# Moving layer 1's embedding products from the end of layer 0's attention to the start of layer 1's latent attention

## The chip, the cores and the metric

The kernel is one program on one core of a Trainium2 chip. The metric is device microseconds (us) of one execution, start to end. The core has five engines with a queue of instructions each: TensorE (PE; its weight loads are shown as PEld), VectorE (DVE), ScalarE (ACT), GpSimd (POOL) and SyncE (SP), which issues every DMA of this kernel.

## The reference

A trunk of two layers over 1024 tokens of width 1024. Layer 0 mixes with pooling and differential attention (six heads), layer 1 with latent attention (C, four heads) and a gated delta rule (D, four heads, chunks). After each mixer stands a gated embedding term:

```python
for i in range(DEPTH):
    hn = rmsnorm(h, norm_g[i])
    m = even_layer(hn, ...) if i % 2 == 0 else odd_layer(hn, ...)
    h = h + m
    h = h + jax.nn.sigmoid(h @ ple_w_gate[i]) * (p[i] @ ple_w_proj[i])
```

`p[i] @ ple_w_proj[i]` is the embedding product: 1024 tokens x 256 times 256 x 1024, one for each layer. It depends on inputs alone, so it may be done at any time before the end of its layer. In D each chunk needs the inverse of a unit triangular matrix:

```python
a_mat = eye + where(strict, kk * gamma * beta, 0)
sol = triangular_solve(a_mat, rhs, lower=True, unit_diagonal=True)
```

## The kernel before

Every product of weights and activations is three float32r matmuls (high by high, high by low, low by high parts; `mm3`, L142 to L144), so that the result is near float32. Weights come by DMA into one of 4 buffers named `raw`, ACT casts the high part `wh` (L134) and DVE subtracts for the low part `wl` (L135). Results gather in PSUM banks: two named `acc`, two `s`, two `x`, one `tr`, one `o`.

The program is written as generators that are stepped in turn; a scheduler then fixes at build time one order for every engine's queue. Each engine runs its queue in that order, and an instruction that waits holds up all behind it. Names of tiles carry a number for each use; the profile leaves the numbers out.

The stages that matter here, in order:

- Layer 0's attention heads. Beside the last head, `ple_both` makes the embedding products of both layers, 16 results of 128x512 for each layer, every one six matmuls. Each is copied from its bank into a tile `z` (L127 on ACT, L129 on DVE) and stored in DRAM as `ple` (L590). What is left when the head ends is drained by `step(*[ahead] * 32)`. Then `out_stage` (layer 0) takes the heads' results `cat` and the weights `w_out`; its first product waits for the last head, the weights and the banks.
- Layer 1's projections, `gdn_prep` (chunk matrices L into DRAM), and `gate_proj(1)` (`gp1`): eight gate products of 24 matmuls each, evacuated by ACT (L896) and DVE (L897).
- `block_solve`: 31 columns of 32x32 triangular inverses, one chain of 62 dependent DVE operations (L979, L981), whose result goes to DRAM as `xinv` (L982).
- `mla_prep(0)`: transposes of the first latent head's q and k (L1127, eight banks of four), each copied by ACT (L1128) and subtracted by DVE (L1129).
- `mla_attn` (C: scores L1144 to L1148, softmax L261 and L265, values L272) interleaved with `gdn` (D): `gdn_solve` loads `U` from `xinv` (L995), transposes it on DVE (L1005 to L1007) and finishes each inverse with small matmuls (L1012 to L1041); `gdn_half` runs the recurrence (L1073 to L1079).

Of the kernel before, what the change touches and what calls it, by code (L numbers as in the profile page):

```python
# [10 lines left out]
F32 = mybir.dt.float32  # L11
F32R = mybir.dt.float32r
# [9 lines left out]
P = 128  # L22
# [34 lines left out]
def trunk_kernel(ctx, tc, a, out, layers=2):  # L57
    nc = tc.nc
    v, s, g, pe, dma = nc.vector, nc.scalar, nc.gpsimd, nc.tensor, nc.sync
# [3 lines left out]
    wp = ctx.enter_context(tc.tile_pool(name="weights", bufs=9))  # L63
# [3 lines left out]
    pools = {}  # L67

    def nm(p):
        uid[0] += 1  # L70
        return f"{p}{uid[0]}"

    def open_pool(name, side="left"):
        st = ExitStack()
        p = st.enter_context(tc.tile_pool(name=name, bufs=1, side=side, reuse_waits="tile"))
        return st, p

    def T(tag, bufs, shape=(512,), dt=F32, pool=None, parts=P):
        return (pool or pools["y"]).tile([parts, *shape], dt, tag=tag, bufs=bufs, name=nm(tag))
# [4 lines left out]
    def bank(tag):  # L84
        return pp.tile([P, 512], F32, tag=tag, bufs=BANKS[tag], name=nm(tag))

    def xt():
        return T("x", 32, dt=F32R, pool=pools["x"])
# [35 lines left out]
    def copy(i, out_, in_):  # L124

        if i % 2 == 0:
            s.copy(out_, in_)  # L127
        else:
            v.tensor_copy(out_, in_)  # L129

    def split(hi, lo, src, scale=None):

        if scale is None:
            s.copy(hi, src)  # L134
            v.tensor_tensor(out=lo, in0=src, in1=hi.bitcast(F32), op=ALU.subtract)  # L135
        else:
            s.activation(hi, src, AF.Identity, scale=scale)
            v.scalar_tensor_tensor(out=lo, in0=src, scalar=scale, in1=hi.bitcast(F32),
                                   op0=ALU.mult, op1=ALU.subtract)
# [6 lines left out]
    def stage(src):  # L146
        raw = wp.tile([P, 512], F32, tag="raw", bufs=4, name=nm("raw"))
        dma.dma_start(raw, src)
        return raw

    def wload(ap, c0, n, nk=KC):

        res = []
        for k in range(nk):
            raw = wp.tile([P, 512], F32, tag="raw", bufs=4, name=nm("raw"))[:, :n]
            hi = wp.tile([P, 512], F32R, tag="hi", name=nm("wh"))[:, :n]
            lo = wp.tile([P, 512], F32R, tag="lo", name=nm("wl"))[:, :n]
            dma.dma_start(raw, ap[k * P:(k + 1) * P, c0:c0 + n])
            split(hi, lo, raw)
            res.append((hi, lo))  # L160
        return res
# [9 lines left out]
    def proj_T(act, w, j, h, ps, order=None):  # L171
        sl = slice(j * P, j * P + P)
        ks = order or list(range(len(w)))
        for i, k in enumerate(ks):
            xh, xl = act[k][h]
            mm3(ps, w[k][0][:, sl], w[k][1][:, sl], xh, xl, i == 0, i == len(ks) - 1)
# [115 lines left out]
    ple = [scratch("ple0"), scratch("ple1")]  # L292
# [52 lines left out]
    for k in range(KC):  # L345
        load_x(0, k, sums)
        raw = stage(a["ev_w_in"][k * P:(k + 1) * P, 0:512])
        hi, lo = [wp.tile([P, 512], F32R, tag=n, name=nm(n)) for n in ("hi", "lo")]
# [14 lines left out]
    for j, n in enumerate(("x", "x", "tr", "acc")):  # L363
        ps = bank(n)
# [202 lines left out]
        finish(1)  # L567
        yield

    def ple_both():  # L570

        for layer in range(layers):
            slots = [xt() for _ in range(8)]
            pT = [[None, None] for _ in range(2)]
            for h in range(2):
                for k in range(2):
                    hi, lo = slots[4 * h + 2 * k], slots[4 * h + 2 * k + 1]
                    split(hi, lo, stage(a["pT"][layer, k * P:(k + 1) * P, h * 512:(h + 1) * 512]))
                    pT[k][h] = (hi, lo)
            for gq in range(2):  # L580
                if gq == 0:
                    yield
                w = wload(a["ple_w_proj"][layer], 512 * gq, 512, nk=2)
                for j in range(4):
                    t = T("z", 2, (2, 512))
                    for h in range(2):
                        ps = bank("acc")
                        proj_T(pT, w, j, h, ps)
                        copy(h, t[:, h], ps)
                        dma.dma_start(ple[layer][4 * gq + j][h], t[:, h])  # L590
                    yield

    def fresh():
        return dict(Q=[], K=[], V=[], G=[])
# [1 line left out]
    def step(*gens):  # L596
        for it in gens:
            next(it, None)

    st = fresh()  # L600
    ahead = even_proj(0, st)
# [6 lines left out]
    for hd in range(6):  # L608
        at, late = even_attn(hd, st), ahead
        if hd < 5:  # L610
            st = fresh()
            ahead = even_proj(hd + 1, st)
        else:
            ahead = ple_both()
        step(at, at, ahead, late, done, at, at, ahead, at, at, ahead, at, ahead, at, at)
        done = at
    step(done)
# [115 lines left out]
    gq = row(ip, "gq", a["od_q_norm"].rearrange("o d -> (o d)"), 192)  # L733
# [234 lines left out]
    def block_solve(nt):  # L968

        xf = T("nx", 2, (1024,), pool=bp)  # L970
        N, X = [t.rearrange("p (j i) -> p j i", j=32) for t in (nt, xf)]
        tm = T("tm", 1, (256,), pool=bp)
        g.memset(xf, 0.0)
        g.memset(xf[:, 0:1024:33], 1.0)
        for j in range(31):

            nr, ncol = j + 1, 31 - j
            t = tm[:, 0:nr * ncol].rearrange("p (a i) -> p a i", a=nr)
            v.tensor_tensor(out=t, in0=X[:, 0:nr, j:j + 1].to_broadcast([P, nr, ncol]),  # L979
                            in1=N[:, j:j + 1, j + 1:32].to_broadcast([P, nr, ncol]), op=ALU.mult)  # L980
            v.tensor_tensor(out=X[:, 0:nr, j + 1:32], in0=X[:, 0:nr, j + 1:32], in1=t, op=ALU.subtract)  # L981
        dma.dma_start(xinv, xf)  # L982
# [126 lines left out]
            s.activation(ct, tr, AF.Identity, scale=onorm)  # L1109
            dma.dma_start(cat[1][4 + hd][h], ct)  # L1110

    def mla_prep(hd, st):
        for h in range(2):
            zq, zk = T("zq", 2, (4, 256), pool=mp), T("zq", 2, (4, 256), pool=mp)

            Q, K, V = T("Q", 3, (3, 512), F32R, mp), T("K", 3, (4, 512), F32R, mp), T("V", 4, pool=mp)
            for n, t in (("Q", Q), ("K", K), ("V", V)):
                st[n].append(t)
            dma.dma_start(zk, qkv[h][:, :, hd, 256:512])
            dma.dma_start(zq, qkv[h][:, :, hd, 0:256])  # L1120
            dma.dma_start(c3(V), qkv[h][:, :, hd, 512:640])
            yield
            for z, lo, dst, hb, lb, part in ((zk, 0, K, 2, 3, slice(0, P)), (zk, P, K, 0, 1, slice(0, P)),
                                             (zq, 0, Q, 1, 2, slice(0, P)), (zq, P, Q, 0, 0, slice(64, P))):
                ps = bank("acc")
                for c in range(4):
                    pe.transpose(ps[:, c * P:(c + 1) * P], z[:, c, lo:lo + P], ident)  # L1127
                s.copy(dst[:, hb, :], ps)  # L1128
                v.tensor_tensor(out=dst[part, lb, :], in0=ps[part], in1=dst[part, hb, :].bitcast(F32), op=ALU.subtract)  # L1129
            yield  # L1130
# [50 lines left out]
    w = wload(w_in, 0, 456)  # L1181
# [11 lines left out]
    qkvs, gp0, gp1 = both(), gate_proj(0), gate_proj(1)  # L1193
# [3 lines left out]
    nt = T("nx", 2, (1024,), pool=bp)  # L1197
    prep = iter(())
    for hd in range(H):
        w, zps = wload(w_in, 456 + 384 * hd, 384), []  # L1200
        for h in range(2):
            outs = []
# [1 line left out]
            step(cv, prep, cv, prep, cv, prep, prep)  # L1204
            prep = gdn_prep(hd, h, *outs)
    step(gp1, prep, gp1, prep, gp1, prep, prep)
    block_solve(nt)
    istack.close()
    istack, mp = open_pool("mla")
    PW[0], PBUFS[1] = T_, 1  # L1210
    PBUFS[0] = 2
    st = dict(Q=[], K=[], V=[])
    ahead = mla_prep(0, st)
    step(ahead, gp1, gp1, ahead, ahead, gp1, gp1, ahead, gp1)
    bstack.close()
    xstack.close()
    sstack, pools["scan"] = open_pool("scan", "right")
    astack, pools["y"] = open_pool("attn")

    def gdn():  # L1220
        parts = [(pair, h, {}) for pair in ((0, 1), (2, 3)) for h in range(2)]
        yield from gdn_load(*parts[0])
        for n, part in enumerate(parts):
            ahead = gdn_load(*parts[n + 1]) if n < 3 else iter(())
            for i, _ in enumerate(gdn_half(*part)):
                if i in (1, 3):
                    step(ahead)
                yield
        sstack.close()

    rec = gdn()
    for hd in range(H):
        at = mla_attn(hd, st)
        st = dict(Q=[], K=[], V=[])
        ahead = mla_prep(hd + 1, st) if hd < H - 1 else iter(())
        for i in range(9):
            step(at, rec)
            if i % 3 == 2:
                step(rec)
            if i in (3, 4, 6, 7):  # L1240
                step(ahead)
# [73 lines left out]
```

## Time and profile before

| | us |
|---|---|
| median of 3 runs | 1497.71 (1496.02 to 1498.46) |
| the profiled execution | 1490.0, its span 1488.3 |
| PE busy | 1419.7 (95% of the span), mean granted clock 0.99 |
| DVE busy | 1000.5 (67%) |
| ACT busy | 655.7 (44%) |
| embedding products drained after the last head of layer 0 | about 531 to 555 |
| `block_solve` on DVE | 1074.4 to 1104.5 |
| first softmax of the latent attention | 1105.5 |

Times within the span are us from its start. Most of the span PE has no gap; the page's slices show where it has. A row of the timeline reads: start, duration, engine, line, operation, output<-input, shape, count, and in brackets the idle time before it with what ended that. Matmul durations overlap: the distance between starts is what a stream of them costs.

### The profile page before, as it was taken

Reading aid. Unit: us, or ns where it says so; the run is one execution under the profiler, and the core shown is the slowest. Engines: PE = TensorE matmul, PEld = TensorE weight load, DVE = VectorE, ACT = ScalarE, POOL = GpSimd, SP = SyncE. Lnnn points to the kernel's source line nnn. Section 1 sums busy time; section 2 is a strip of 40 time slices with the busy share of each in tenths; the row PEclk is TensorE's granted clock in tenths of the full one; section 3 lists DMA queues with packets and bytes.
Section 4 is the critical chain, followed back from the end, with each engine's and each line's share of the span. In section 5 each row is a group of like instructions: output and inputs, shape, how many; then the busy total and the mean of one; then the engine's idle time right before and its main releaser. Section 6 shows DMA issues by size and latency. Waiting matters only on the chain. (4 is left out here: it accounts for less than half of the span.)

```text
span 1488.3 us, 22788 instructions
## 1 busy us (share of the span) xinstructions
PE 1419.7 (95%) x7494; PEld 1158.3 (78%) x7494; DVE 1000.5 (67%) x2939; ACT 655.7 (44%) x1642; POOL 206.2 (14%) x347
## 2 busy tenths in 40 slices
PE   7799999999999999999998999999889999999998
PEld 6578887888888778887886777888768788887786
DVE  7855666676767857356669789888577888643342
ACT  4415555565566751234454434444223446722220
POOL 3430101010101001012104441110000000000021
PEclk9999999999999999999999999999989999999999
DMA  5315233232335483334323442343455644353332
GB/s 166 95 51 141 56 101 79 78 90 68 100 86 148 134 276 94 107 120 152 118 41 131 167 154 99 99 133 123 138 162 183 212 140 149 114 156 99 120 114 85
DMA packets 131557, 181.52 MB, mean 122 GB/s; under 512 B 32496, under 2 KB 59248, under 8 KB 131440
## 3 DMA queue, kind: packets, MB, share of 16 engines
q1 hardware_dynamic: 131440, 180.08, 39.7%
q8 instruction: 59, 0.97, 0.3%
q14 instruction: 58, 0.48, 0.1%
HBM read 108.20 MB, written 52.95 MB: 108 GB/s over the span
## 5 line engine op out<-in xcount | busy, mean ns | idle before, releaser
L142 PE MATMUL acc<-wh,x 128*128 128x512 f32 (+1 forms) x576 | 231.6, 402 | 2.3 <-DVE g L454 1.9
L143 PE MATMUL acc<-wl,x 128*128 128x512 f32 (+1 forms) x576 | 229.9, 399 | 3.0 <-DVE wl L135 3.0
L144 PE MATMUL acc<-wh,x 128*128 128x512 f32 (+1 forms) x576 | 228.5, 397 | 0.0
L144 PE MATMUL acc<-x,wl 128*128 128x512 f32 x512 | 204.5, 400 | 3.3 <-DVE wl L135 3.3
L142 PE MATMUL acc<-x,wh 128*128 128x512 f32 x512 | 204.8, 400 | 1.9 <-ACT wh L134 0.9
L143 PE MATMUL acc<-x,wh 128*128 128x512 f32 x512 | 203.0, 397 | 0.0
L134 ACT CAST wh<-raw 128x512 fp32r<-128x512 f32 (+2 forms) x176 | 101.3, 599 | 80.2 <-PE acc L143 25.6
L135 DVE TENSOR_TENSOR wl<-raw,wh 128x512 fp32r<-128x512 f32 (+2 forms) x176 | 114.9, 674 | 28.6 <-ACT wh L134 25.9
L143 PEld LDWEIGHTS acc<-wl,x 128*128 128x128 f32 x576 | 109.4, 190 | 27.1 <-DVE wl L135 4.5
L142 PEld LDWEIGHTS acc<-wh,x 128*128 128x128 f32 x576 | 109.3, 190 | 25.7 <-issue 2.8
L144 PEld LDWEIGHTS acc<-wh,x 128*128 128x128 f32 x576 | 109.2, 190 | 22.3
L144 PEld LDWEIGHTS acc<-x,wl 128*128 128x128 f32 x512 | 96.5, 188 | 27.9 <-DVE wl L135 5.9
L142 PEld LDWEIGHTS acc<-x,wh 128*128 128x128 f32 x512 | 96.4, 188 | 25.0 <-ACT wh L134 1.3
L265 ACT ACTIVATE p<-p,mx 128x128 f32<-128x128 f32 (+7 forms) x128 | 99.4, 777 | 33.0 <-DVE mx L261 24.3
L143 PEld LDWEIGHTS acc<-x,wh 128*128 128x128 f32 x512 | 96.3, 188 | 21.5
L669 POOL TENSOR_TENSOR u<-hp,hp 128x512 f32<-128x512 f32 x32 | 43.5, 1358 | 486.9 <-DVE hp L135 205.7
L144 PE MATMUL acc<-hp,wl 128*128 128x512 f32 x256 | 101.6, 397 | 0.4 <-DVE wl L135 0.4
L143 PE MATMUL acc<-hp,wh 128*128 128x512 f32 x256 | 101.5, 396 | 0.0
L142 PE MATMUL acc<-hp,wh 128*128 128x512 f32 x256 | 101.4, 396 | 0.0
L261 DVE CUSTOM_DVE_ANT_0 p<-s,cst 128x512 f32<-128x512 f32 (+3 forms) x128 | 74.2, 586 | 29.2 <-PE s L523 15.6
L667 DVE SCALAR_TENSOR_TENSOR th<-th,ld 128x512 f32<-128x512 f32 x32 | 28.8, 899 | 73.7 <-ACT th L665 73.7
L450 ACT ACTIVATE z<-acc,rstd 128x256 f32<-128x256 f32 x48 | 22.7, 474 | 112.2 <-PE acc L144 112.2
(462 smaller groups left out, 2906.1 us busy)
## 6 DMA issues: line engine op xcount, KB each, us to landing
raw<-in_ev_w_in SPq DMA_DIRECT2D x56, 256.0 KB
Q<-sq SPq DMA_DIRECT2D x96, 128.0 KB
qkv<-zz SPq DMA_DIRECT2D x16, 640.0 KB
raw<-cat SPq DMA_DIRECT2D x32, 256.0 KB
ple<-z SPq DMA_DIRECT2D x32, 256.0 KB
raw<-in_ple_w_gate SPq DMA_DIRECT2D x32, 256.0 KB
ld<-ple SPq DMA_DIRECT2D x32, 256.0 KB
zq<-qkv SPq DMA_DIRECT2D x16, 512.0 KB
```

The costliest lines, as they stand in the source:

```text
L134: s.copy(hi, src)
L135: v.tensor_tensor(out=lo, in0=src, in1=hi.bitcast(F32), op=ALU.subtract)
L142: pe.matmul(ps, lh, rh, start=first, stop=False)
L143: pe.matmul(ps, lh, rl, start=False, stop=False)
L144: pe.matmul(ps, ll, rh, start=False, stop=last)
L261: v.tensor_tensor_reduce(out=pm[:, c * 512:c * 512 + n], in0=ps[:, 0:n], in1=mk, scale=-scale, scalar=prev, op0=ALU.add, op1=ALU.min, accu ...
L265: s.activation(pm[:, 0:w], pm[:, 0:w], AF.Exp, bias=prev, scale=-1.0, accum_out=sums)
L450: s.activation(z[:, t % 4, :], ps[:, 0:256], AF.Identity, scale=rstd[0][:, t:t + 1])
L667: v.scalar_tensor_tensor(out=th, in0=th, scalar=1.0, in1=r, op0=ALU.add, op1=ALU.mult)
L669: g.tensor_tensor(out=u, in0=hi.bitcast(F32), in1=lo.bitcast(F32), op=ALU.add)
```

## The change

`ple_both` becomes `ple_proj(layer, slot, outs)`. Layer 0's products stay beside the last head, with a `z` tile for each result: two results in flight where there were four. Layer 1's products become `fill`. Its first step (four loads of `pT`, split into a pool `embed` of their own) is stepped before `block_solve`; its eight others are stepped after the last gate product, with the first two `gdn_load` (two `gdn_solve`) called among them. Only then is the pool `attn` of the latent attention opened, in memory that `embed` has given back. Layer 1's results are copied by ACT alone, into the four `raw` buffers that weights and `pT` use too. `mla_prep(0)` takes the banks `s` and `x` by turns (four) in place of `acc` (two), and its steps are spread among the gate products.

```diff
-    def ple_both():
-        for layer in range(layers):
-            slots = [xt() for _ in range(8)]
...
-                    t = T("z", 2, (2, 512))
+    def ple_proj(layer, slot, outs):
+        pT = [[None, None] for _ in range(2)]
+        for h in range(2):
+            for k in range(2):
+                hi, lo = slot(), slot()
+                split(hi, lo, stage(a["pT"][layer, k * P:(k + 1) * P, h * 512:(h + 1) * 512]))
+                pT[k][h] = (hi, lo)
+        yield
+        for gq in range(2):
+            w = wload(a["ple_w_proj"][layer], 512 * gq, 512, nk=2)
+            for j in range(4):
+                for h in range(2):
+                    ps, t = bank("acc"), outs()
+                    proj_T(pT, w, j, h, ps)
+                    copy(h * (1 - layer), t, ps)
+                    dma.dma_start(ple[layer][4 * gq + j][h], t)
+                yield
...
-            ahead = ple_both()
+            ahead = ple_proj(0, xt, lambda: T("z", 2, (2, 512))[:, 0])
...
-    def mla_prep(hd, st):
+    def mla_prep(hd, st, banks=("acc",)):
...
-                ps = bank("acc")
+                ps = bank(banks[nb % len(banks)])
+                nb += 1
...
-    block_solve(nt)
     istack.close()
     istack, mp = open_pool("mla")
+    fstack, fp = open_pool("embed")
+    fill = ple_proj(1, lambda: T("pT", 8, dt=F32R, pool=fp), lambda: wp.tile([P, 512], F32, tag="raw", bufs=4, name=nm("ple")))
+    step(fill)
+    block_solve(nt)
...
-    ahead = mla_prep(0, st)
-    step(ahead, gp1, gp1, ahead, ahead, gp1, gp1, ahead, gp1)
+    ahead = mla_prep(0, st, ("s", "x"))
+    step(ahead, gp1, gp1, ahead, gp1, ahead, gp1, ahead, gp1)
...
-    astack, pools["y"] = open_pool("attn")
...
     rec = gdn()
+    step(fill, fill, rec, fill, fill, fill, rec, fill, fill, fill)
+    fstack.close()
+    astack, pools["y"] = open_pool("attn")
```

In the changed kernel the lines from `mla_prep` on are two lower (L1125 are its transposes, L1127 its subtractions), those from `out_stage` to `gdn_half` four lower (L893 for L897, L975 and L977 for L979 and L981, L1008 for L1012).

What moves in the queues, at three places. First PE, from the last gate products on. Before, `acc_11570` and `acc_11599` are the fourth and fifth gate product, 24 matmuls each; `zq` are the first head's k and q:

```order
L144 MATMUL acc_11570<-wh_11302,x_7604 128x512
L142 MATMUL acc_11599<-wh_11260,x_7269 128x512
...
L144 MATMUL acc_11599<-wh_11302,x_7788 128x512
L1127 MATMUL acc_11628<-cst,zq_11563 128x128 x4
L1127 MATMUL acc_11635<-cst,zq_11563 128x128 x4
...
L142 MATMUL acc_11664<-wh_11260,x_7269 128x512
...
L272 MATMUL o_11901<-V_11566,pt_11904 128x128
L1012 MATMUL acc_11830<-wk_11816,L_11804 32x32
L1147 MATMUL s_11992<-K_11565,Q_11564 128x384
```

Now `acc_11528` is the seventh gate product and `acc_11585` the eighth, `acc_11631` the first embedding result, `acc_11661` the fourth, `acc_11754` the fifth:

```order
L144 MATMUL acc_11528<-wh_11110,x_7596 128x512
L1125 MATMUL s_11463<-cst,zq_11398 128x128 x4
L1125 MATMUL x_11470<-cst,zq_11398 128x128 x4
...
L142 MATMUL acc_11585<-wh_11068,x_7077 128x512
...
L142 MATMUL acc_11631<-pT_11306,wh_11620 128x512
...
L144 MATMUL acc_11661<-pT_11324,wl_11627 128x512
L1146 MATMUL s_11993<-K_11400,Q_11399 128x256
L1008 MATMUL acc_11697<-wk_11683,L_11671 32x32
...
L1037 MATMUL acc_11742<-U_11672,kw_11680 128x128 x4
L142 MATMUL acc_11754<-pT_11306,wh_11620 128x512
```

The first transposes stood behind five gate products and now stand behind seven. The first solve (L1012, now L1008) stood among attention matmuls and now stands ahead of twelve of the sixteen embedding results.

Second DVE, inside `block_solve` (`tm` and `nx` are its tiles). Before, seven columns in:

```order
L981 TENSOR_TENSOR nx_11491<-nx_11491,tm_11492 128x6x26
L979 TENSOR_TENSOR tm_11492<-nx_11491,nx_9539 128x175
L1129 TENSOR_TENSOR K_11565<-acc_11628,K_11565 128x512
L981 TENSOR_TENSOR nx_11491<-nx_11491,tm_11492 128x7x25
L1129 TENSOR_TENSOR K_11565<-acc_11635,K_11565 128x512
```

Now:

```order
L977 TENSOR_TENSOR nx_11330<-nx_11330,tm_11331 128x6x26
L1127 TENSOR_TENSOR K_11400<-s_11463,K_11400 128x512
L975 TENSOR_TENSOR tm_11331<-nx_11330,nx_9347 128x175
L1127 TENSOR_TENSOR K_11400<-x_11470,K_11400 128x512
L977 TENSOR_TENSOR nx_11330<-nx_11330,tm_11331 128x7x25
```

The subtraction of the first transposed bank stands at the same column as before, one operation earlier.

Third DVE, at the end of layer 0's last head (L546 scales the head's last output `o`, which PE then transposes on L553; `wl` are `w_out`'s low parts). Before:

```order
L543 TENSOR_TENSOR ony_5895<-ony_5895,hrstd_149 128x4
L546 SCALAR_TENSOR_TENSOR o_5588<-o_5588,ony_5895,g_5018 128x128 x4
L135 TENSOR_TENSOR wl_6301<-raw_6299,wh_6300 128x512
L129 COPY z_6007<-acc_6017 128x512
L135 TENSOR_TENSOR wl_6307<-raw_6305,wh_6306 128x512
```

Now:

```order
L135 TENSOR_TENSOR wl_6121<-raw_6119,wh_6120 128x512
L543 TENSOR_TENSOR ony_5898<-ony_5898,hrstd_149 128x4
L135 TENSOR_TENSOR wl_6127<-raw_6125,wh_6126 128x512
L546 SCALAR_TENSOR_TENSOR o_5589<-o_5589,ony_5898,g_5018 128x128 x4
L129 COPY z_6005<-acc_6004 128x512
```

Four of `w_out`'s subtractions that stood behind L546 now stand ahead of it (the last two are shown).

More of the change, by code (lines that the diff above doesn't have):

```diff
@@ L568, in even_attn @@
         yield
-    def ple_both():
-        for layer in range(layers):
-            slots = [xt() for _ in range(8)]
[L574 to L584, printed above, removed]
-                    t = T("z", 2, (2, 512))
-                    for h in range(2):
-                        ps = bank("acc")
[L588 to L591, printed above, removed]
+    def ple_proj(layer, slot, outs):
[15 more added lines that the diff above has]
+                yield
     def fresh():
@@ L1110, in gdn_half @@
             dma.dma_start(cat[1][4 + hd][h], ct)
-    def mla_prep(hd, st):
+    def mla_prep(hd, st, banks=("acc",)):
+        nb = 0
         for h in range(2):
@@ L1124, in mla_prep @@
                                              (zq, 0, Q, 1, 2, slice(0, P)), (zq, P, Q, 0, 0, slice(64, P))):
-                ps = bank("acc")
+                ps = bank(banks[nb % len(banks)])
+                nb += 1
                 for c in range(4):
```

## The prediction, before the run

> **What bounds the kernel now.** I read the page first: busy shares and slices, for where PE, the busiest engine, has room.
>
> ```profile
> PE 1419.7 (95%) x7494; PEld 1158.3 (78%) x7494; DVE 1000.5 (67%) x2939; ACT 655.7 (44%) x1642; POOL 206.2 (14%) x347
> PE   7799999999999999999998999999889999999998
> ```
>
> PE is the bound nearly everywhere, so moving products helps only if they leave a place where PE is full and land where it is empty. The place they leave, by stretches of PE's work on the tile `acc` (columns: stretch, length, busy, count, clock, DMA share, GB/s), and the first product of the output stage from PE's timeline:
>
> ```profile
> 531.80:555.10 23.30, 22.83 (x97) 1.00 0.83 276
> 555.17 0.50 PE L142 MATMUL acc<-x,wh 128*128 128x512 f32 x1 [0.51 <-ACT z L127]
> ```
>
> From the last head's end to the output stage PE does 96 or so embedding matmuls without a gap, at full clock. That is layer 1's share, and it can go. The place they go to, by PE's timeline, and by stretches of all engines (length, then PE, PEld, DVE, ACT, POOL busy with counts, clock, DMA share, GB/s):
>
> ```profile
> 1061.56 0.48 PE L142 MATMUL acc<-wh,x 128*128 128x512 f32 x1
> 1072.88 0.60 PE L1127 MATMUL acc<-cst,zq 128*128 128x128 f32 x4
> 1074.54 0.66 PE L1127 MATMUL acc<-cst,zq 128*128 128x128 f32 x4 [1.06 <-DVE gz L897]
> 1078.92 1.97 PE L1127 MATMUL acc<-cst,zq 128*128 128x128 f32 x8 [3.72 <-DVE K L1129]
> 1105.88 0.44 PE L1144 MATMUL s<-K,Q 128*128 128x384 f32 x1 [1.71 <-DVE mx L261]
> 1110.62 0.80 PE L272 MATMUL o<-V,pt 128*128 128x128 f32 x2 [3.54 <-DVE r L1152]
> 1111.34 0.31 PE L1012 MATMUL acc<-wk,L 32*32 32x32 f32 x2
> 1072.80:1081.70 8.90, 4.12 (x22) 3.20 (x20) 7.10 (x22) 2.92 (x5) 0.00 (x0) 0.70 0.51 160
> 1104.20:1111.30 7.10, 1.80 (x6) 1.05 (x6) 2.54 (x15) 1.93 (x6) 0.00 (x0) 0.71 0.83 237
> 1116.30:1160.00 43.70, 42.32 (x459) 35.94 (x457) 33.48 (x146) 17.35 (x37) 3.33 (x8) 1.00 0.61 189
> 1160.00:1306.00 146.00, 141.22 (x1162) 123.78 (x1162) 113.22 (x449) 83.20 (x182) 1.69 (x4) 1.00 0.49 153
> ```
>
> PE is empty for 4.8 of 8.9 us around the first transposes and for 5.3 of 7.1 us before the first solve, some 10 us. After 1116 it is full again (42.3 of 43.7). So the room is under half of the products' time, and whether even that is used hangs on the queues. The chain through this place runs on DVE and SP, by their timelines:
>
> ```profile
> 1074.40 0.18 DVE L979 TENSOR_TENSOR tm<-nx,nx 128x31 f32<-128x31 f32 x1
> 1077.92 0.34 DVE L979 TENSOR_TENSOR tm<-nx,nx 128x175 f32<-128x175 f32 x1
> 1078.18 0.68 DVE L1129 TENSOR_TENSOR K<-acc,K 128x512 fp32r<-128x512 f32 x1
> 1104.27 0.21 DVE L981 TENSOR_TENSOR nx<-nx,tm 128x31 f32<-128x31 f32 x1
> 1104.55 0.33 SPq L982 DMA_DIRECT2D xinv<-nx  x1
> 1107.29 0.32 SPq L995 DMA_DIRECT2D U<-xinv  x1
> 1105.53 0.28 DVE L261 CUSTOM_DVE_ANT_0 p<-s,cst 128x128 f32<-128x128 f32 x1
> 1109.35 0.42 DVE L261 CUSTOM_DVE_ANT_0 p<-s,cst 128x256 f32<-128x256 f32 x1 [3.52 <-DMA gate<-gz]
> ```
>
> `block_solve` holds DVE for 30.1 us (1074.40 to 1104.48). From its end to the first solve matmul on PE pass 6.8 us (1104.55 to 1111.34): store, load of `U`, transposes on DVE.
>
> **The change part by part.** The unit: the fourth and fifth gate products are 48 matmuls and take 11.32 us (1061.56 to 1072.88), so 0.236 each; a gate product is 5.66, an embedding result of six 1.41, layer 1's sixteen 22.6 us.
>
> *Early, what is removed.* 22.6 us of PE leave the drain. Late next is the last head's end. DVE now has four more subtractions of `w_out` ahead of L546, by the listings.
>
> ```profile
> 530.58 1.14 DVE L546 SCALAR_TENSOR_TENSOR o<-o,ony,g 128x128 f32<-128x128 f32 x4
> 531.08 0.50 PE L553 MATMUL tr<-cst,o 128*128 128x128 f32 x2
> 531.64 0.68 DVE L135 TENSOR_TENSOR wl<-raw,wh 128x512 fp32r<-128x512 f32 x1
> 533.59 0.32 SPq L590 DMA_DIRECT2D ple<-z  x1
> 536.90 0.59 ACT L127 COPY z<-acc 128x512 f32<-128x512 f32 x1 [2.78 <-DMA ple<-z]
> ```
>
> At 0.6 us each (their distance when queued) L546 starts about 2.4 us later, at 533, and L553 at 533.6. One embedding result stands behind it (1.4), and its bank and the next wait for copies into `z`: a store holds its tile for 3.3 us (533.59 to 536.90), and with two results in flight instead of four that is 4.0 us for two results where PE needs 2.8, so the last ones wait about 1 us. The output stage then starts near 536.0 instead of 555.2: a gain of 19.2. Bounds: 22.6 if neither costs anything; 15 if the staging of `cat` and `w_out`, at a DMA share of 0.83 in this stretch, is late by another 4. The second half of `cat` and the loads of x are needed only from the third product chain on, 11 us later, and are covered by it; without that cover they would cost up to 4, the same bound.
>
> *Late, the DVE wait.* PE now runs four gate products before the first transposes: 1061.56 + 4 x 5.66 = 1084.2. Transposes, ACT's copy and the queue bring the first subtraction L1127 to 1085.4. DVE reaches it after the twelfth operation of `block_solve` (1078.3) and one subtraction of `pT` (0.6), at 1078.9, and stands for 6.5 us with all the rest of the inverse behind it. From there before took 26.3 us (1078.18 to 1104.48) with eight subtractions and two gate evacuations in it; now one more evacuation and two `wl` (three times 0.6), less about 1 us of small waits that go, so 27.1. `block_solve` ends at 1112.6, plus 6.8: the first solve can start at 1119.4. If the stall were nothing it would be 1112.9.
>
> *Late, what PE has until then.* After 1084.2: transposes 4.0, a wait for the `acc` bank of the sixth gate product (ACT evacuates it only behind four casts, DVE behind four subtractions) about 2.5, the eighth gate product 5.7, four embedding results 5.7, ten score matmuls 1.7: until 1104. The other twelve results stand behind L1008 in PE's queue, so PE is empty for 15.4 us. The four banks for the transposes cost nothing and gain the two waits of 1.06 and 3.72, but only where PE is not waiting for more; they are in the sum through these times.
>
> *Late, the solves.* Before, solves ran with attention matmuls between their steps; now nothing stands between.
>
> ```profile
> 1123.36 0.21 PE L1012 MATMUL acc<-wk,L 32*32 32x32 f32 x1
> 1129.95 1.06 PE L1041 MATMUL acc<-U,kw 128*128 128x128 f32 x8
> 1121.37 2.05 PE acc L1041 x16
> 520.40 0.44 SPq L158 DMA_DIRECT2D raw<-in_ev_w_out  x1
> 523.76 0.62 ACT L134 CAST wh<-raw 128x512 fp32r<-128x512 f32 x1 [0.46 <-DMA raw<-in_ev_w_out]
> ```
>
> A solve takes 7.5 us from end to end (1123.36 to 1130.9), of which PE works about 4 (estimate: L1041 2.05, the three smaller steps together as much). So: first solve 7.5; four results 5.7 and 1 for the clock after the wait; two recurrence matmuls 0.5; then two results whose weights come late. Their `raw` buffers are the tiles of the results just stored: one store (3.3), one load to cast (3.4, 520.40 to 523.76), cast and subtraction 1.3, in all 8 us after the first copy, so 5.8 us pass for 2.8 us of work; second solve 7.5; six results 8.5. That is 36.5 us: the fill ends at 1155.9. The ends: 25.7 if PE waits for nothing, 42 if each solve takes 9 and the weights 3 more.
>
> *Late, who waits.* Attention's pool is opened in `embed`'s memory, and DVE's first softmax stands behind all of this. It starts at 1155.9 instead of 1105.5: 50.4 later. Given back: two solves are done (2 x 4 of PE, which is full from there on), and the 3.5 us that the second softmax waited for a gate's store. Lag 38.9. Eight copies go from DVE to ACT, 0.59 each (the row at 536.90); ACT is busy for 17.4 of 43.7 us after 1116 and has that room, without it they would cost 4.7. SP's queue gets layer 1's 24 transfers: two `pT` loads stand ahead of the last load for `block_solve`, 0.9 us at 0.44 an issue, covered because the inverse starts behind the fifth gate product (done 1072.9) anyway, else 0.9; the stores of the first four results are issued before 1105, ahead of `xinv`'s turn. POOL's order is unchanged.
>
> The rest of the attention, full before (141.2 of 146), can give back a few us at most; I take none. Sum: 38.9 - 19.2 = +19.7 on the profiled 1490.0, so 1509.7. The profiled execution is 7.7 below the median of the runs; on the median 1497.7 it is 1517.4.
>
> The clock beside this:
>
> ```profile
> 1082.16 0.63 PE L143 MATMUL acc<-wl,x 128*128 128x512 f32 x1
> 1082.58 0.63 PE L144 MATMUL acc<-wh,x 128*128 128x512 f32 x1
> 1083.36 0.40 PE L143 MATMUL acc<-wl,x 128*128 128x512 f32 x1
> 1083.59 0.39 PE L144 MATMUL acc<-wh,x 128*128 128x512 f32 x1
> ```
>
> After the gap that ended at 1078.92 matmuls came 0.42 apart, by 1083.36 0.23 apart: some 4 us at near half rate, 2 lost. I take half of it after the long wait, since the solve itself covers the rest. The Trainium skill, "TensorE: Matmul & The Clock Gate", Part 1, has the array at half rate after an idle window of about 3.4 us, until about 3.4 us of work. By that rule the long wait costs 1.7 and the sum is 0.7 higher; the trace agrees with it here. The same page asks for no gaps of over 3 us between bursts, and by that the change, which puts products into a gap, should win: that is the first rival.
>
> **The rivals.**
>
> *The queue's order does not bind, and PE never runs dry (faster).* Place: L1008. The price is the plain work: 1084.2 + 4.0 + 5.7 + 22.6 + 1.7 + 8 + 1 = 1127.2 for the fill's end; lag 1127.2 - 1105.5 - 8 - 3.5 = 10.2, less 19.2 gives -9, so 1488.7. It needs L1008 to start by about 1106 and something to run between the solves' steps; with the rest packed, each us of later start costs one, and the sign turns at 1115. Against it: `block_solve` cannot end before 1078.9 + 27.1 = 1106 even without the stall, and the 6.8 follow.
>
> *All follow-on waits are small (no change).* No stall on DVE (-6.5), solves at PE's 4 us (-7), weights in time (-3), no clock loss (-1), the full 22.6 early (-3.4): 19.7 - 20.9 = -1.2, 1496.5. For it: ACT and DMA have room. Against it: it needs all five.
>
> *The early gain is not had.* The drain covers the staging of the output stage (DMA 0.83); if that then binds, only 15 less a further wait remain: with a gain near 3 the sum is +36, 1534. Against it: `cat` loads move ahead of the head's end in SP's queue, and four of w_out's weights are split before L546.
>
> **How the numbers follow.** Likeliest, 0.72: slower by 19.7, own range +9 (half of the five savings) to +30 (early 15, solves 9, no softmax wait given back): 1507 to 1528. First rival 0.13, second 0.09, third 0.06. A measurement here tells about 0.2%, 3 us, from nothing. Faster: the first and a little of the second, 0.15; the same: most of the second, 0.06; slower: 0.79. The range 1490 to 1529 leaves out most of the third and the lower half of the first, about 0.13, and what nobody listed.
>
> **What would show it.** Right: PE's first output product near 536; DVE idle some 6 us before the first L1127; `xinv` stored near 1112 - 19; PE idle over 10 us before the first L1008; first softmax near 1156 - 19. Wrong: L1008 starting within 2 us of the scores before it, or the solves' steps taking 4 us. A wait at the output stage's first product, with DMA as releaser, would speak for the third rival.

## The result and the profile after

The changed kernel takes 1513.31 us (median of 4 runs, 1512.56 to 1514.02), the kernel before 1496.87 (4 runs, 1492.54 to 1498.46). The ratio is 1.0114, with a 95% interval of 1.0092 to 1.0137: slower by 16.4 us. The profiled execution takes 1512.76 us with a span of 1511.0, against 1490.0 and 1488.3 before.

The page's busy row and PE's slices:

```profile
PE 1424.3 (94%) x7494; PEld 1163.0 (77%) x7494; DVE 996.6 (66%) x2931; ACT 660.6 (44%) x1650; POOL 205.1 (14%) x347
PE   7799999999999899999999999999659999999998
```

The same number of matmuls, and a hole in two slices (6 and 5, from 1058 to 1133 us) where before stood 8 and 8. The hole by stretches (length, busy time and count of PE, PEld, DVE, ACT, POOL, granted clock, DMA share, GB/s):

```profile
1085.70:1099.80 14.10, 0.02 (x1) 0.01 (x1) 7.39 (x26) 0.00 (x0) 0.00 (x0) 0.65 0.85 289
1099.80:1110.50 10.70, 7.21 (x72) 6.37 (x72) 4.89 (x30) 0.59 (x1) 0.31 (x1) 0.51 0.62 186
1110.50:1116.80 6.30, 6.30 (x31) 5.04 (x29) 1.44 (x12) 2.70 (x5) 0.53 (x1) 1.00 0.45 140
1116.80:1125.90 9.10, 4.39 (x13) 3.21 (x13) 1.68 (x3) 2.40 (x6) 0.00 (x0) 0.81 0.35 105
1125.90:1134.25 8.35, 5.74 (x72) 5.21 (x73) 2.27 (x7) 0.99 (x2) 0.30 (x1) 0.80 0.26 94
1134.25:1142.70 8.45, 8.45 (x39) 6.87 (x38) 1.91 (x15) 3.52 (x6) 0.53 (x1) 1.00 0.38 132
```

In this order: PE stands empty; the first solve; four results; two results with late weights; the second solve; six results. Only the stretches with results alone are full. The events, by the timelines of PE and DVE:

```profile
535.05 0.40 PE L142 MATMUL acc<-x,wh 128*128 128x512 f32 x1
545.38 0.68 DVE L645 TENSOR_TENSOR t<-acc,ld 128x512 f32<-128x512 f32 x1
1064.61 0.60 PE L1125 MATMUL s<-cst,zq 128*128 128x128 f32 x4
1065.99 0.69 DVE L1127 TENSOR_TENSOR K<-s,K 128x512 fp32r<-128x512 f32 x1 [7.14 <-ACT K L1126]
1069.74 1.09 PE L1125 MATMUL s<-cst,zq 128*128 128x128 f32 x4 [3.23 <-DMA zq<-qkv]
1093.35 0.21 DVE L977 TENSOR_TENSOR nx<-nx,tm 128x31 f32<-128x31 f32 x1
1099.52 0.48 DVE L1001 STREAM_TRANSPOSE wk<-U 32x32 f32<-32x32 f32 x4 [5.96 <-DMA U<-xinv]
1099.82 0.28 PE L1008 MATMUL acc<-wk,L 32*32 32x32 f32 x2 [14.10 <-issue]
1121.00 0.80 PE L142 MATMUL acc<-pT,wh 128*128 128x512 f32 x1 [4.19 <-ACT wh L134]
1142.24 0.29 DVE L261 CUSTOM_DVE_ANT_0 p<-s,cst 128x128 f32<-128x128 f32 x1 [3.95 <-PE acc L144]
```

DVE waits 7.14 us for the late transposes with most of `block_solve` behind it; PE then waits 14.10 us for `block_solve`'s result (through the load of `U` and its transposes on DVE) with twelve of the sixteen results behind L1008; the first softmax comes at 1142.24, behind all of them. Its row ends on one of the last product matmuls (`<-PE acc L144`): the pool `attn` lies in memory that the products' operands hold until then, so no softmax runs beside PE's gap either.

One measure serves for all that follows: the late stage, from the last `gdn_prep` product (`x<-cq,ck`) to latent attention's last gated output (`og`), by the groups of these tiles (count, min/median/max in ns, first and last start). Before, then after:

```profile
L948 PE MATMUL x<-cq,ck x64: 274/275/276, 910.9 to 1061.5; 128*128 128x128 f32 x64
L1162 DVE SCALAR_TENSOR_TENSOR og<-o,r,gt x32: 330/350/352, 1112.0 to 1302.6; 128x128 f32<-128x128 f32 x32
```
```profile
L944 PE MATMUL x<-cq,ck x64: 275/275/275, 891.6 to 1042.0; 128*128 128x128 f32 x64
L1160 DVE SCALAR_TENSOR_TENSOR og<-o,r,gt x32: 338/350/353, 1146.9 to 1325.8; 128x128 f32<-128x128 f32 x32
```

It is 241.1 us before and 283.8 after: 42.7 more. A second profiled execution of the changed kernel gives 285.1, so this measure repeats to about 1 us. What comes behind it (185 to 186 us) and what lies between the output stage's first subtraction and it (494 to 498) is the same in every kernel here. The way up to that subtraction is not so steady: 545.38 in one execution of the changed kernel, 540.93 in the other.

### The profile page after: what moved, and what is told of

It reads as the page before. It is cut to its first block, busy times and chain, and to the rows that moved or that the text cites. A ratio compares the mean times of both kernels' runs of the same rounds, so it can differ in the third digit from the quotient of the medians.

```text
span 1511.0 us, 22755 instructions
## 1 busy us (share of the span) xinstructions
PE 1424.3 (94%) x7494; PEld 1163.0 (77%) x7494; DVE 996.6 (66%) x2931; ACT 660.6 (44%) x1650; POOL 205.1 (14%) x347
## 4 chain that ended last, share of the span: by engine, by line
PE 68%; DVE 15%; DMA 7%; ACT 6%; issue 3%; POOL 1%; SPq 0%; DVEq 0%; ACTq 0%; POOLq 0%
PE acc L144 16%; PE acc L142 16%; PE acc L143 16%; PE o L272 4%; PE s L522 1%; PE tr L279 1%; DVE wl L135 1%; PE s L523 1%; DVE p L261 1%; PE acc L1037 1%; DMA raw<-in_xT 1%; DMA raw<-in_ev_w_in 1%; DMA raw<-cat 1%; ACT p L265 1%; PE x L944 1%
## 5 line engine op out<-in xcount | busy, mean ns | idle before, releaser
L144 PE MATMUL acc<-wh,x 128*128 128x512 f32 (+1 forms) x576 | 228.1, 396 | 0.0
L142 PE MATMUL acc<-x,wh 128*128 128x512 f32 x480 | 192.9, 402 | 2.5 <-ACT z L127 1.1
L144 PE MATMUL acc<-x,wl 128*128 128x512 f32 x480 | 192.2, 401 | 3.1 <-DVE wl L135 3.1
L143 PE MATMUL acc<-x,wh 128*128 128x512 f32 x480 | 190.1, 396 | 0.0
L144 PEld LDWEIGHTS acc<-wh,x 128*128 128x128 f32 x576 | 109.1, 189 | 22.5
L265 ACT ACTIVATE p<-p,mx 128x128 f32<-128x128 f32 (+7 forms) x128 | 99.4, 777 | 33.3 <-DVE mx L261 22.6
L144 PEld LDWEIGHTS acc<-x,wl 128*128 128x128 f32 x480 | 90.5, 189 | 26.5 <-DVE wl L135 5.7
L142 PEld LDWEIGHTS acc<-x,wh 128*128 128x128 f32 x480 | 90.7, 189 | 24.3 <-DVE z L129 1.3
L143 PEld LDWEIGHTS acc<-x,wh 128*128 128x128 f32 x480 | 90.6, 189 | 20.6
L144 PE MATMUL acc<-hp,wl 128*128 128x512 f32 x256 | 101.2, 395 | 0.0
L663 DVE SCALAR_TENSOR_TENSOR th<-th,ld 128x512 f32<-128x512 f32 x32 | 32.4, 1014 | 72.6 <-ACT th L661 72.5
L450 ACT ACTIVATE z<-acc,rstd 128x256 f32<-128x256 f32 x48 | 22.8, 475 | 112.1 <-PE acc L144 112.0
```

Source lines behind the costliest of these rows:

```text
L142: pe.matmul(ps, lh, rh, start=first, stop=False)
L143: pe.matmul(ps, lh, rl, start=False, stop=False)
L144: pe.matmul(ps, ll, rh, start=False, stop=last)
L265: s.activation(pm[:, 0:w], pm[:, 0:w], AF.Exp, bias=prev, scale=-1.0, accum_out=sums)
L450: s.activation(z[:, t % 4, :], ps[:, 0:256], AF.Identity, scale=rstd[0][:, t:t + 1])
L663: v.scalar_tensor_tensor(out=th, in0=th, scalar=1.0, in1=r, op0=ALU.add, op1=ALU.mult)
```

## The experiments

Theory: the loss is one of order in PE's queue. The products stand behind a solve that cannot start, the solves run with nothing between their steps, and the weights of the last products come late. Rivals: the products are slow in this place whatever stands around them; or the reordered transposes cost the time, not the products. A part of the theory is left untested: no run gives attention memory of its own, so what it loses by the pool alone is not known.

All times, each ratio to the kernel before in the same comparison (its median lay between 1490.3 and 1496.9 in the four comparisons), and the late stage:

| kernel | us | ratio, 95% interval | late stage |
|---|---|---|---|
| before | 1496.87 | 1 | 241.1 |
| changed | 1513.31 | 1.0114 (1.0092 to 1.0137) | 283.8 |
| changed, again (e9) | 1511.01 | 1.0118 (1.0096 to 1.0141) | 285.1 |
| no layer 1 products (e1) | 1473.75 | 0.9875 (0.9840 to 0.9909) | 247.1 |
| all results ahead of the solves (e2) | 1489.07 | 0.9979 (0.9960 to 0.9999) | 261.7 |
| transposes in two banks (e3) | 1505.34 | 1.0083 (1.0057 to 1.0110) | 278.7 |
| e2 and e3 (e4) | 1494.03 | 1.0010 (0.9991 to 1.0028) | 267.0 |
| weights first (e5) | 1506.25 | 1.0101 (1.0074 to 1.0128) | 278.6 |
| weights first, again (e10) | 1504.17 | 1.0070 (1.0049 to 1.0091) | 279.4 |
| e2, weights first (e6) | 1481.91 | 0.9934 (0.9910 to 0.9959) | 253.2 |
| e6, mixed banks (e7) | 1482.01 | 0.9937 (0.9913 to 0.9960) | 254.7 |
| e7, z by halves (e8) | 1477.46 | 0.9910 (0.9890 to 0.9931) | 255.7 |
| changed, z by halves (e11) | 1508.32 | 1.0097 (1.0076 to 1.0117) | 284.1 |
| e6, z by halves (e12) | 1476.95 | 0.9896 (0.9873 to 0.9919) | 253.5 |

**e1: the products left out.**

```diff
-                    dma.dma_start(r, ple[layer][jj][h])
+                    dma.dma_start(r, ple[0][jj][h])
...
-    step(fill)
     block_solve(nt)
...
-    step(fill, fill, rec, fill, fill, fill, rec, fill, fill, fill)
+    step(rec, rec)
```

> Layer 1's embedding products are left out altogether (the output stage adds layer 0's embedding again), the rest is as in the changed kernel. It splits the result into its early and its late half. Theory (the solve blocks PE's queue): the early gain stays, the output stage's first product near 533 as in the changed kernel, and 19 us against the kernel before; the stall on VectorE before the first subtraction stays near 7 us, but attention's matmuls run beside the solves again, so the late part costs under 5 us: 1475 to 1485 us. Rival (the reordered transposes and the later inverse are what costs, not the products): most of the late loss of 36 us remains without them: 1495 to 1512.

The time was just under the theory's range. The late stage is 6.0 us longer than before, not under 5, and 36.7 shorter than with the products. So 22.6 us of matmuls cost 36.7 in the new place, and the transposes and the late inverse alone cost 6.0. DVE and PE of this kernel:

```profile
1062.83 0.69 DVE L1127 TENSOR_TENSOR K<-s,K 128x512 fp32r<-128x512 f32 x1 [7.50 <-ACT K L1126]
1089.53 0.69 PE L1142 MATMUL s<-K,Q 128*128 128x384 f32 x1 [13.36 <-DVE mx L261]
```

The stall on DVE is there, and PE stands 13.36 us for the softmax behind it: this is the gap that products could fill. The first softmax follows `block_solve` at once here (1089.18 behind 1089.06), where in the changed kernel it came 48.7 us behind it. The rival that it is the transposes falls, for 36.7 of the 42.7.

**e2: all sixteen results ahead of the solves.**

```diff
-    step(fill, fill, rec, fill, fill, fill, rec, fill, fill, fill)
+    step(*[fill] * 8, rec, rec)
```

> Nothing is left out; all sixteen results stand ahead of the two solves in PE's queue, and the solves run beside attention. Theory (queue order): the 14 us in which PE stood before the first solve are filled, the solves' own waits (10.7 and 8.4 us for some 4 us of PE work each) are covered by attention, and the weights' wait stays: the first softmax comes near 1106 instead of 1142, of which some 8 us go back for the solves' work and some for the recurrence: 1485 to 1497 us. Rival (the products are limited in this stretch by their weights, stores and the DMA share of 0.85, whatever stands around them): the results run no faster than the solves allowed before, and at most 10 us are won: 1503 to 1513.

The time is in the theory's range; the late stage falls by 22.1 us and the kernel is about as fast as before. The rival that the products are slow in this place falls. The edit fills the gap ahead of the first solve and puts both solves beside attention; how the 22.1 divides between the two is not shown. PE's stretch with both solves, the waits that are left, and SP's queue ahead of the second:

```profile
1108.30:1125.50 17.20, 16.66 (x194) 13.86 (x194) 12.76 (x57) 7.14 (x19) 1.19 (x4) 1.00 0.73 235
```
```profile
1068.33 1.09 PE L1125 MATMUL s<-cst,zq 128*128 128x128 f32 x4 [3.39 <-DVE nx L977]
1094.08 0.79 PE L142 MATMUL acc<-pT,wh 128*128 128x512 f32 x1 [4.11 <-ACT wh L134]
1107.74 0.29 DVE L261 CUSTOM_DVE_ANT_0 p<-s,cst 128x128 f32<-128x128 f32 x1
```
```profile
1085.42 1.72 SPq L586 DMA_DIRECT2D ple<-ple  x2
1088.22 0.32 SPq L586 DMA_DIRECT2D ple<-ple  x1
1089.04 0.33 SPq L158 DMA_DIRECT2D raw<-in_ple_w_proj  x1
1089.62 0.32 SPq L586 DMA_DIRECT2D ple<-ple  x1
1090.15 0.33 SPq L158 DMA_DIRECT2D raw<-in_ple_w_proj  x1
```

Beside attention both solves pass in 17.2 us in which PE is busy for 16.66 at clock 1.00; alone they took 10.70 and 8.35 at 0.51 and 0.80. The wait of 4.11 ends with a cast of weights whose loads were issued at 1089.04 and 1090.15, among the stores of results that hold the four `raw` buffers.

**e3: the transposes through the two acc banks again; e4: that and e2.**

```diff
-    ahead = mla_prep(0, st, ("s", "x"))
+    ahead = mla_prep(0, st)
```

> Only the transposes' four banks are undone: they go through the two acc banks again, and stand after two gate products in PE's queue, not four. Theory (the stall on VectorE is on the path, because block_solve ends it): the 7.1 us before the first subtraction go, block_solve ends about 6 us earlier, the first solve starts near 1094 instead of 1099.8, and all behind it moves: 1505 to 1509 us. Rival (PE's own work is the limit there, and the waits for two banks of 1.06 and 3.72 us come back): no change, 1511 to 1516.

> Both edits: all sixteen results ahead of the solves, transposes through the two acc banks after two gate products. Theory (queue order): PE has work until about 1105 either way, so the earlier end of block_solve is worth little here, only the last eight results' weights, which VectorE subtracts behind block_solve, come earlier: 0 to 5 us better than the version with four banks. Rival (the stall adds wherever the products stand): the full 6 to 7 us better than it.

One edit, two signs: e3's time is in the theory's range and its late stage 5.1 us shorter than the changed kernel's; e4's late stage is 5.3 longer than e2's, where the theory had expected up to 5 less and the rival 6 to 7 less. Both expectations of e4 were wrong. The rows that tell why, of e3, then of e4:

```profile
1057.60 0.68 DVE L1127 TENSOR_TENSOR K<-acc,K 128x512 fp32r<-128x512 f32 x1
1090.50 0.22 PE L1008 MATMUL acc<-wk,L 32*32 32x32 f32 x2 [0.46 <-issue]
```
```profile
1055.94 1.98 PE L1125 MATMUL acc<-cst,zq 128*128 128x128 f32 x8 [4.58 <-DVE K L1127]
1097.78 0.80 PE L142 MATMUL acc<-pT,wh 128*128 128x512 f32 x1 [4.12 <-ACT wh L134]
```

In two banks the transposes stay behind two of the gate products that follow `gdn_prep`, not four; DVE does not stall (no wait in the row at 1057.60), and the solve starts sooner: 50.4 us behind the last `gdn_prep` product, 57.8 in the changed kernel. But PE waits in the middle of the transposes for their banks (4.58). In e4 PE came to its wait for the last weights 56.0 us behind that product, in e2 49.6, so e4's loss lies ahead of that wait. The reading that fits both: where PE waits for the solve anyway, as in the changed kernel, the earlier inverse counts; where PE has results to do until then, only its own waits count.

**e5, e10: all weights ahead of the first result.**

```diff
+        both = [wload(a["ple_w_proj"][1], 512 * gq, 512, nk=2) for gq in range(2)] if layer else None
         for gq in range(2):
-            w = wload(a["ple_w_proj"][layer], 512 * gq, 512, nk=2)
+            w = both[gq] if layer else wload(a["ple_w_proj"][layer], 512 * gq, 512, nk=2)
```

> The changed kernel, but layer 1's four weight tiles of the embedding are all loaded and split ahead of its first result, not the last two of them behind the first eight results. Theory (the last weights come late because their staging tiles are held by results on their way out, and PE waits for that between the two solves): the two results between the solves take 2.8 us instead of 8.8, and little else moves: 4 to 6 us faster than the changed kernel, 1507 to 1509.5. Rival (the second solve waits for its own inputs anyway, or two more subtractions inside block_solve delay the first solve by as much): 1511 to 1515.

> The changed kernel with all four of layer 1's weight tiles ahead of its first result, beside the changed kernel itself. Theory (late weights cost PE some 6 us between the solves, and what is won there reaches the end): 4 to 6 us faster than it. Rival (attention takes most of it back, since it waits for other things then): 0 to 2 us.

e5's time is just under the theory's range, but it cannot be told from the changed kernel, whose ratio came from another comparison: the intervals overlap. So the changed kernel and e10 were compared directly:

> The changed kernel once more, unaltered, so that the two small edits that follow are compared with it on one chip. Both theories: 1.009 to 1.013 of the kernel before.

There it is 6.8 us faster (1511.01 to 1504.17), a little more than the theory's 4 to 6, and the late stage 5.7 shorter: the late weights are on the path.

**e6, e7: both edits, and mixed banks** (`("acc", "s", "x", "o")` in place of `("s", "x")`).

> All sixteen results ahead of the solves, and all four weight tiles ahead of the first result. Theory (late weights): PE's wait of 4.1 us in the middle of the results and the 1 to 2 us at low clock behind it go: 1482 to 1486 us. Rival (the later matmuls only wait elsewhere, for the copies or for the first softmax on VectorE): 1487 to 1491, as without this edit.

> As the one before, and the transposes' four banks are acc, s, x and o, so that the first of each four stands in its place behind two gate products, not four, and the other three need not wait for a bank. Theory (the two banks cost PE some 7 us of waits where it is full, 4.58 + 0.64 + 0.24 + 0.51 + 0.24 and the low clock; four late ones cost it a wait of 3.4): PE keeps most of its time, and 2 to 4 us are won: 1479 to 1484. Rival (early transposes wait for VectorE's turn in block_solve, whichever banks they have, as with two banks): no gain or up to 4 us lost, 1484 to 1490.

e6: the late stage is 8.5 us shorter than e2's, and the kernel is now faster than the one before, just under the theory's range. e7's time is in its theory's range, but it was a miss all the same, since the 2 to 4 us that were to be won on e6 are not there: the transposes are early and DVE's stall is gone, but PE now waits as long for a gate's bank as it waited in e6 for the second half's `zq` (3.07 in both):

```profile
1072.79 0.50 PE L142 MATMUL acc<-wh,x 128*128 128x512 f32 x1 [3.07 <-DVE gz L894]
```

**e8, e11, e12: layer 0's results in both halves of z by turns.**

```diff
+            zh = []
+
+            def half():
+                if not zh:
+                    t = T("z", 2, (2, 512))
+                    zh.extend((t[:, 1], t[:, 0]))
+                return zh.pop()
-            ahead = ple_proj(0, xt, lambda: T("z", 2, (2, 512))[:, 0])
+            ahead = ple_proj(0, xt, half)
```

> As the one before, and layer 0's results alternate between both halves of z, so that four are in flight early, as in the kernel before, not two. Theory (the two waits of 0.8 and 1.05 us for copies in the first drain come from two results in flight): the output stage's first product comes 1 to 2 us earlier, and the time is 1 to 2 us less than without this edit. Rival (the start of the output stage waits for o's scale on VectorE and for its staging next): within 0.5 us.

> The changed kernel with layer 0's results in both halves of z by turns, four in flight. Theory (two in flight cost the first drain its waits for copies, 0.8 and 1.05 us, and the products behind them stand later in PE's order): 1 to 4 us faster than the changed kernel, all of it before the output stage's first subtraction from the residual. Rival (o's scale on VectorE sets the start): within 0.5 us.

> All results ahead of the solves, all weights ahead of the first result, and z by halves; the transposes' banks as in the changed kernel. Theory (the three edits take away separate waits, and the mixed banks made no difference): 0.989 to 0.993 of the kernel before. Rival (with z by halves, the transposes' stall on VectorE comes onto the path, which the mixed banks had taken away): 0.994 to 0.997.

e11 is 2.7 us faster than e9 (no run of one reaches into the runs of the other, though the intervals of their ratios overlap), e8 4.5 faster than e7, more than the 1 to 2 expected; the late stages differ by 1.0 at most. The waits for `z` are gone from PE. Where e11 wins its 2.7 us is not shown: the output stage's first subtraction stands at 540.84 in its profiled execution and at 540.93 in e9's. What is left ahead of the output stage in e11 is

```profile
531.41 0.50 PE L553 MATMUL tr<-cst,o 128*128 128x128 f32 x2 [1.29 <-DVE o L546]
```

e12 has the order, the weights and `z` together: 0.9896 of the kernel before, in the theory's range and 17.7 us faster than the kernel before in the same comparison. In its late stage layer 1's products cost 6.4 us (253.5 against 247.1 without them) for their 22.6 of work. DVE's stall of 7.14 us is still there, and costs little under a full PE: e8, which has no such stall, is no faster (0.9910).

```profile
1059.16 0.69 DVE L1135 TENSOR_TENSOR K<-s,K 128x512 fp32r<-128x512 f32 x1 [7.14 <-ACT K L1134]
1062.00:1078.00 16.00, 15.02 (x62) 12.54 (x63) 14.72 (x32) 6.69 (x11) 1.03 (x3) 0.79 0.85 275
1078.00:1100.00 22.00, 21.79 (x104) 17.37 (x102) 12.17 (x50) 10.09 (x22) 0.00 (x0) 1.00 0.84 284
```

## Why the prediction was right, and where its terms were not

The sign and the mechanism held: products behind the waiting solve, attention behind all of them. The size held too, 1517 forecast and 1513.31 measured, but with some luck, since terms missed in both directions (see the sum). Predicted times of the late stage are moved by 19.5 us, the lead at the last `gdn_prep` product (1061.5 to 1042.0).

- *Early gain, 19.2.* The output stage's first product came at 535.05 (forecast 536.0), its first subtraction from the residual 19.4 us earlier than before (564.80 to 545.38). The sum is right, its parts less so. L546 began at 530.97, 0.4 later than before and not 2.4: the four subtractions did lengthen DVE's chain from the head's norm (L121) to it, 5.53 us where it was 2.69, but the head came to L121 2.5 sooner (525.44, before 527.89). PE did wait for copies into `z`, but twice (0.82 and 1.05), and with e9's 540.93 the term is known to some 4 us only.
- *DVE's wait, 6.5.* 7.14. The end of `block_solve`, 1093.1 by the forecast, was 1093.56; the first solve, 1099.9, began at 1099.82. PE's gap, 15.4, was 14.10. This chain is the core of the theory, and e3 confirms that the stall feeds it.
- *A wait of 2.5 for the sixth gate product's bank.* Not there; PE waited 3.23 us for the second half's `zq` instead. Near in size by luck, wrong in cause.
- *Solves, 7.5 each.* 10.70 and 8.35: the step that was mis-sized most, by 4.0 together. The rows that 7.5 came from had attention beside them and a clock of 1.00; alone, the first solve ran at 0.51. But 7.5 was also the shortest of the first four solves of the kernel before: the first, beside attention too, took 12.1 (1111.34 to the end of its last L1041, whose row stands below this list). So the runs do not show that a solve takes longer alone; they show that alone it keeps PE from other work, 19.05 us for both. The forecast put 1 us of low clock behind the solve, on the four results; those ran at 1.00 (6.30 busy of 6.30).
- *Two results with late weights, 5.8.* 9.10, 3.3 more: the loads were issued at 1116.09 and 1118.37, each behind stores of the results just made, and a stretch at half rate followed the wait.
- *End of the results, 1136.4 by the forecast.* 1142.7, later by 6.3: 4.0 + 3.3 - 1.0.
- *Given back, 11.5.* The first softmax stood 100.2 us behind the last `gdn_prep` product, 44.0 before, so 56.2 later; at the stage's end 42.7 are left, so 13.5 were given back. The lag is 42.7 where 38.9 was forecast.
- *The sum.* +19.7 on 1490.0 gave 1509.7; the profiled execution took 1512.76. On the medians the difference is 16.4, not 22.8, because the profiled execution before lies 6.9 us below the median there and the one after only 0.6. The forecast added 7.7 for that to both, so its terms fell 3 us short on the profile and its time came out 4 us too high on the medians. That both are small is in part luck: the results ended 6.3 too late, 2.0 more were given back, and the two profiled executions stand differently to their medians.

```profile
1122.37 1.06 PE L1041 MATMUL acc<-U,kw 128*128 128x128 f32 x8
```

Of the rivals, "PE never runs dry" needed L1008 at 1106 in the time of before; it began at 1099.8 + 19.5 = 1119.3, past its turning point of 1115. What it described is what e6 and e12 reach by another order: a faster kernel. "The early gain is not had" is refuted by 545.38. "All follow-on waits are small" is refuted by the six rows of stretches above. How much each part of the loss costs by itself depends on the others: order 22.1 us of the late stage (e2), weights 5.7 alone (e10) and 8.5 on top of it (e6), banks 5 in either direction (e3, e4).

## What to carry to other kernels

Work that is moved into a gap fills it only if it stands ahead of the instruction that waits: read from the order what is queued behind the wait, and put the filling work in front of it and latency-bound chains beside other work. Take a chain's duration from several rows (here 7.5 to 12.1 us for the first four solves), and its clock from one in which it has the company that it will have. Look, too, whose memory the moved work holds: here the softmax behind it had to wait for that. An edit that saves a wait on one engine (banks, transposes) has its sign from which engine is short in that stretch, so try it again after each larger edit.

## What the runs showed of the hardware

PE's clock stayed low through nearly all of the first solve: 0.51 over 10.70 us, though PE was busy for 7.21 of them, with waits of 0.4 to 1.4 us between groups of short matmuls. At the low clock eight 64x64 products took 1.08 us, at the full one in the second solve 0.65:

```profile
1104.10 1.08 PE L1025 MATMUL acc<-wk,L 64*64 64x64 f32 x8 [1.35 <-DVE wk L1021]
1128.57 0.65 PE L1025 MATMUL acc<-wk,L 64*64 64x64 f32 x8 [1.07 <-DVE wk L1021]
1130.92 2.07 PE L1037 MATMUL acc<-vb,U 128*128 128x128 f32 x8 [0.51 <-DVE U L1031]
```

Then the second solve, too, fell to the low clock (1.00 from 1128.50 to 1130.40, 0.51 from 1130.90 to 1134.25): its L1037 took 2.07 us for what took 1.05 beside attention in e2:

```profile
1114.30 1.05 PE L1037 MATMUL acc<-vb,U 128*128 128x128 f32 x8
```

The Trainium skill, "TensorE: Matmul & The Clock Gate", Part 1, has the array at full rate after about 3.4 us of sustained work. Behind the wait of 4.19 us the trace agrees: matmuls came 0.42 us apart from 1121.60 on and 0.23 apart from 1124.06, 3.1 us after the start. In the first solve 4.03 us of work in the 7.50 from 1099.80 to 1107.30, in short pieces, did not do it (clock 0.50); behind 3.18 us of L1037 without a wait, from 1110.50 on, it was 1.00.
